# A different order of weight pairs and a different tail in the last chunk of a hybrid encoder block

## The chip, the cores and the metric

The kernel runs as one program on one core of a Trainium2 chip. The metric is the device time of one execution in microseconds (us). Three runs of the kernel before gave 1358.62, 1359.98 and 1359.87 us, with a median of 1359.87 us. One more execution was profiled. Its own time is 1359.19 us, and the trace of it spans 1357.4 us.

## The reference, cut to what matters

The reference is one encoder block on x of 256 tokens by 2048 channels, all in float32. Its last step, the only one that the change touches, is the second half of the feed-forward network, the residual sum and a final RMS norm:

```python
h = _rmsnorm(x, norm_ffn_g[l])
gate, up = jnp.split(jnp.einsum('bsd,df->bsf', h, w_ffn_in[l]), 2, axis=-1)
x = x + jnp.einsum('bsf,fd->bsd', jax.nn.silu(gate) * up, w_ffn_out[l])
...
def _rmsnorm(x, g):
    y = x32 * lax.rsqrt(jnp.mean(x32 * x32, axis=-1, keepdims=True) + EPS)
    return (y * g.astype(F32)).astype(x.dtype)
```

Here w_ffn_out has 5632 rows and 2048 columns. The mean of squares of the final norm goes over the 2048 channels of each token, so no output can be scaled before the last column of its token is summed.

## The kernel before, in words

**Number format.** Every float32 weight is split into two parts: `whi`, a rounded copy made by ScalarE (L68), and `wlo`, the rest, made by VectorE (L69). The activations H were split in the same way earlier. One product is then three matmuls of 128x512 into one PSUM bank: high by high, high by low and low by high (L283 and L284). The middle one needs `wlo`, the other two need only `whi`. The three add into one bank and stand in that order.

**Halves, pairs and lookahead.** Weights come from memory in halves of 128x1024. `Net.take(i)` hands out half i and first has halves up to i + 5 loaded and split (L130 to L133, AHEAD = 3 and two more). SP issues the loads. A load waits until its buffer, used six loads earlier, is free. ScalarE and VectorE split each half in the order in which the halves are taken.

**Two kinds of pairs.** A pair j stands for 2 x 128 rows of the weights. `Quad` (L261) computes two blocks of 512 output columns for both blocks of 128 tokens (tt = 0 and 1). A *plain* pair has two halves and for each of them four products, one into each of the banks N3, P2, E and Q4 (`plain`, L299): 24 matmuls. The banks P2 and N3 hold the two column blocks of tt = 0, Q4 and E those of tt = 1. A *seven* pair uses seven products in place of eight (a scheme after Strassen): 21 matmuls in four quarters (`seven`, L304), of six, six, six and three. For it VectorE also forms sums of weights, L115 ahead of the first quarter, L120 ahead of the second and L124 ahead of the third, besides the four splits L69, the last of them half as wide. Three of the seven products go to the same banks P2, N3 and Q4, and four to banks of their own, P1, Q5, P7 and P6. After the last seven pair, `sums` (L320) and `shared` (L638) work these four banks out on VectorE (L326, L327, L328) and add them to the result `yacc` (L641, twice).

**The last chunk.** The output projection runs in two parts of the rows. The second part has ten pairs and is done for two chunks of 1024 columns, n = 0 and n = 1. The chunk n = 1 is the last work of the kernel on TensorE. Its order of pairs stands in `PLAN_OUT` (L386): 0, 2, 1, 4, 5, 3, 7, 8, 6, 9, of which 2, 4, 5, 7 and 8 are seven pairs. The last two, 6 and 9, are kept out of `Quad.run` (tail = 2) and run by L644 to L647: for tt = 0 all of their products, then for tt = 1. During the first pairs of this chunk VectorE has the end of the chunk n = 0 to do as well: L361, L362, twice L631 and twice L635. The program writes these ahead of the weight splits that the chunk n = 1 asks for itself.

**The tail.** For each tt the two banks are added to `yacc` by VectorE (L650), ScalarE squares and sums each block (L651), VectorE reduces three partial sums, scales them and adds EPS (L558, L559), and `rsqrt_cols` (L211) makes the inverse root by nine small VectorE instructions (L217 to L225, three rounds of two at the end). Then four blocks of 512 columns are scaled, two by VectorE (L658) and two by ScalarE (L661), and SP stores each as it is done (L662).

**What sets the order.** Each engine runs its instructions in a fixed order. A planner sets it ahead of time, on the whole by the order in which the program writes the instructions, with later ones moved ahead where the planner reckons the earlier ones are not ready.

Of the kernel before, what the change touches and what calls it, by code (L numbers as in the profile page):

```python
# [9 lines left out]
F32 = mybir.dt.float32  # L10
# [3 lines left out]
ALU = mybir.AluOpType  # L14
AX = mybir.AxisListType

P = 128
L = 256
D = 2048
# [7 lines left out]
EPS = 1e-6  # L27
# [351 lines left out]
def plan(pairs, seven):  # L379

    return [(j, seven.index(j) if j in seven else None) for j in pairs]
# [1 line left out]

PLAN_IN = plan(range(8), (2, 4, 6))
PLAN_OUT = [[plan(range(12), (2, 4, 6, 7, 9, 10))] * 2,
            [plan(p, (2, 4, 5, 7, 8)) for p in (range(10), (0, 2, 1, 4, 5, 3, 7, 8, 6, 9))]]  # L386
CHUNKS = (6, 5)
RAW_BUFS = 4
HL_BUFS = 4
# [4 lines left out]
def build(nc, tc, a):  # L394
    net = Net(nc, tc, a)
# [37 lines left out]
    with ExitStack() as top:  # L433
# [15 lines left out]
        ss = const.tile([P, 2, 2, 4], F32, name="ss")  # L449
# [63 lines left out]
        for n in range(4):  # L513
# [4 lines left out]
            if n == 0:  # L518
# [3 lines left out]
                fx = sd.enter_context(tc.tile_pool(name="fx", bufs=1))  # L522
# [7 lines left out]
            for tt in range(2):  # L530
                y = yt[:, tt, :]
# [22 lines left out]
        def rms(which, tts, cols):  # L554

            n = len(tts)
            ms = fx.tile([P, n], F32, name="ms", bufs=2)
            nc.vector.tensor_reduce(out=ms, in_=ss[:, which, tts[0]:tts[0] + n, 0:cols], op=ALU.add, axis=AX.X)  # L558
            nc.vector.tensor_scalar(out=ms, in0=ms, scalar1=1.0 / D, scalar2=EPS, op0=ALU.mult, op1=ALU.add)  # L559
            return net.rsqrt_cols(fx, ms, n)  # L560
# [3 lines left out]
        for part in range(2):  # L564
            H = HE = None
            for c in range(CHUNKS[part]):
                q = Quad(net, fx, X2, XE, PLAN_IN, fi_first[c + 6 * part])
                pq, ne = q.parts()
                q.run()
                if c == 0:  # L570
                    if part == 0:
                        inner.close()
                        hpool = sd.enter_context(tc.tile_pool(name="hpool", bufs=1, side="right"))
                        nc.vector.tensor_copy(out=r2, in_=rms(0, (0, 1), 4))
                    H = hpool.tile([P, 24, 512], F32R, name="H")
                    HE = hpool.tile([P, 6, 2, 3, P], F32R, name="HE")
                q.finish(pq, ne)
                for tt in range(2):
                    nc.scalar.activation(out=pq[:, tt, :], in_=pq[:, tt, :], func=AF.Silu, scale=r2[:, tt:tt + 1])
                    nc.vector.scalar_tensor_tensor(out=pq[:, tt, :], in0=ne[:, tt, :], scalar=r2[:, tt:tt + 1],  # L580
                                                   in1=pq[:, tt, :], op0=ALU.mult, op1=ALU.mult)

                def to_h(j, pq=pq, H=H, HE=HE, slots=dict(PLAN_OUT[part][0])):
                    def sink(pt):

                        slot = slots[j]
                        flat = pq[:, j % 2, :].rearrange("p (b t) -> p b t", b=2)
                        nc.scalar.copy(out=flat, in_=pt)
                        hi, lo = H[:, 2 * j:2 * j + 2, 0:L], H[:, 2 * j:2 * j + 2, L:2 * L]
                        nc.scalar.copy(out=hi, in_=flat)  # L590

                        def rest():
                            nc.vector.tensor_tensor(out=lo, in0=flat, in1=hi.bitcast(F32), op=ALU.subtract)
                            if slot is not None:
                                forms(net, fx, flat, HE, slot, H, j)
                        net.later(3 + j % 2, rest)
                    return sink
                net.later(4, lambda pq=pq, c=c, f=to_h: net.turn([[pq[:, tt, L * b:L * (b + 1)] for tt in range(2)] for b in range(2)],
                                                                 [f(2 * c + b) for b in range(2)]))
            for n in range(2):  # L600
                end = part == 1 and n == 1
                q = Quad(net, fx, H, HE, PLAN_OUT[part][n], fo_first[2 * part + n], tail=2 if end else 0)
                if part == 1 and n == 0:

                    x2s.close()
                    gfp = sd.enter_context(tc.tile_pool(name="gfp", bufs=1))
                    yacc = gfp.tile([P, 2, D], F32, name="yacc")
                    gB = gfp.tile([P, D], F32, name="gfB")
                    other = [gfp.tile([P, D], F32, name=f"other{tt}") for tt in range(2)]
                    for tt in range(2):  # L610
                        nc.sync.dma_start(out=yacc[:, tt, :], in_=y_d[tt])
                        nc.sync.dma_start(out=other[tt], in_=p_d[tt])
                    nc.sync.dma_start(out=gB, in_=a["gfin"].partition_broadcast(P))
                    for tt in range(2):
                        net.later(9 + 2 * tt, lambda tt=tt: nc.vector.tensor_tensor(out=yacc[:, tt, :], in0=yacc[:, tt, :],
                                                                                    in1=other[tt], op=ALU.add))
                if not end:
                    pq, ne = q.parts()
                    q.run()
                    q.finish(pq, ne)  # L620
                    if part == 0:
                        def store(n=n, pq=pq, ne=ne):
                            for tt in range(2):
                                for h, t in enumerate((pq, ne)):
                                    c = 1024 * n + 512 * h
                                    nc.sync.dma_start(out=p_d[tt, :, c:c + 512], in_=t[:, tt, :])
                        net.later(2, store)
                    else:
                        for h, t in enumerate((pq, ne)):
                            y = yacc[:, :, 512 * h:512 * (h + 1)]  # L630
                            nc.vector.tensor_tensor(out=y, in0=y, in1=t, op=ALU.add)  # L631
                        for tt in range(2):
                            y = yacc[:, tt, 0:1024]
                            nc.scalar.activation(out=other[tt][:, 0:1024], in_=y, func=AF.Square, accum_out=ss[:, 1, tt, 0:1])
                            nc.vector.tensor_tensor(out=y, in0=y, in1=gB[:, 0:1024], op=ALU.mult)  # L635
                    continue

                def shared(q):  # L638
                    for h, t in enumerate((q.t[:, 1:3, :], q.d)):
                        y = yacc[:, :, 1024 + 512 * h:1536 + 512 * h]  # L640
                        nc.vector.tensor_tensor(out=y, in0=y, in1=t, op=ALU.add)  # L641
                q.run(shared)

                ws = [(net.take(q.first[m] + e), 2 * q.plan[m][0] + e) for m in (-2, -1) for e in range(2)]  # L644
                for tt in range(2):
                    for w, k in ws:
                        q.plain(w, k, (tt,))  # L647
                    for h, name in enumerate((("P2", "N3"), ("Q4", "E"))[tt]):
                        y = yacc[:, tt, 1024 + 512 * h:1536 + 512 * h]
                        nc.vector.tensor_tensor(out=y, in0=q.bank[name], in1=y, op=ALU.add)  # L650
                        nc.scalar.activation(out=other[tt][:, 512 * h:512 * h + 512], in_=y, func=AF.Square,  # L651
                                             accum_out=ss[:, 1, tt, 1 + h:2 + h])

                    r = rms(1, (tt,), 3)
                    for m in (0, 2, 1, 3):
                        y = yacc[:, tt, 512 * m:512 * (m + 1)]
                        if m >= 2:
                            nc.vector.scalar_tensor_tensor(out=y, in0=y, scalar=r[:, 0:1], in1=gB[:, 512 * m:512 * (m + 1)],  # L658
                                                           op0=ALU.mult, op1=ALU.mult)
                        else:  # L660
                            nc.scalar.activation(out=y, in_=y, func=AF.Identity, scale=r[:, 0:1])  # L661
                        nc.sync.dma_start(out=a["out"][tt * P:(tt + 1) * P, 512 * m:512 * (m + 1)], in_=y)  # L662


def phase_a(net, const, ev, psa, ysgu, par, gate_d, sgu_v, tiles, tile_first, sa, left):
# [535 lines left out]
```

## Time and profile before

| | |
|---|---|
| median of three runs | 1359.87 us |
| profiled execution, its own time | 1359.19 us |
| span of its trace | 1357.4 us |
| TensorE (PE) busy | 1340.0 us, 99% |
| weight loads (PEld) busy | 1120.6 us, 83% |
| VectorE (DVE) busy | 1164.2 us, 86% |
| ScalarE (ACT) busy | 796.6 us, 59% |
| chunk n = 1, first and last matmul begin | 1289.95 and 1344.93 us |

All times of the trace count from the start of its span. A row of a timeline gives the begin, the duration, engine, line and operation, output and inputs with their shapes, and how many like instructions in a row were merged into it. An instruction's duration reaches a little past the begin of the next one on its engine, so the pace of a sequence is read from begins.

### The profile page before, as it was taken

The page shows a single profiled execution, that of the slowest core. Times are in us where ns is not written, and L with a number is a line of the kernel's source. Part 1 is how long each engine was busy: PE and PEld are TensorE (multiplying, and loading weights), DVE is VectorE, ACT ScalarE, POOL GpSimd, SP SyncE. Part 2 cuts the span into 40 slices and gives each one's busy share as a digit, 9 for nine tenths or more (in the row PEclk, how much of TensorE's full clock was granted, in tenths as well). Part 3 has the DMA queues.
Part 4 walks back from the last instruction along what each step waited for, and adds up shares of the span by engine and source line. Part 5 has one row for each costly group of instructions (what it writes and reads, how often), then busy time and mean ns, then how long its engine had stood idle before and what let it go on. Part 6 is the DMA issues. An engine that isn't in the chain of part 4 may idle for free.

```text
span 1357.4 us, 17857 instructions
## 1 busy us (share of the span) xinstructions
PE 1340.0 (99%) x6389; PEld 1120.6 (83%) x6389; DVE 1164.2 (86%) x1593; ACT 796.6 (59%) x1034; POOL 0.7 (0%) x6
## 2 busy tenths in 40 slices
PE   9999999999999999999999999999999999999996
PEld 7888888888888888888888888888888888888775
DVE  7887789798889666656898999999999989999998
ACT  7665555455555444455666666666665667665654
POOL 0000000000000000000000000000000000000000
PEclk9999999999999999999999999999999999999998
DMA  8775656556555687676556665666767567558643
GB/s 293 253 241 175 190 179 195 178 170 215 159 179 153 213 342 237 186 233 196 188 188 204 203 209 178 202 201 197 245 209 233 194 192 235 184 186 325 210 165 124
DMA packets 90681, 280.25 MB, mean 206 GB/s; under 512 B 10072, under 2 KB 10976, under 8 KB 89952
## 3 DMA queue, kind: packets, MB, share of 16 engines
q1 hardware_dynamic: 88144, 274.84, 62.7%
q10 hardware_dynamic: 2448, 4.27, 0.8%
q8 instruction: 50, 0.82, 0.2%
q14 instruction: 39, 0.32, 0.1%
HBM read 268.58 MB, written 10.49 MB: 206 GB/s over the span
## 4 chain that ended last, share of the span: by engine, by line
PE 92%; DVE 5%; issue 1%; DMA 1%; ACT 1%; SPq 0%; DVEq 0%; ACTq 0%
PE mm L284 19%; PE mg L284 17%; PE aux L284 10%; PE mm L139 9%; PE mg L173 6%; PE mg L174 6%; PE mg L175 6%; PE mm L141 4%; PE mm L174 2%; PE mm L175 2%; PE mm L173 2%; DVE wlo L69 2%; PE aux L790 2%; PE aux L204 1%; DMA raw<-in_wsv 1%
## 5 line engine op out<-in xcount | busy, mean ns | idle before, releaser
L68 ACT CAST whi<-raw 128x1024 fp32r<-128x1024 f32 (+1 forms) x530 | 523.6, 1002 | 428.1 <-PE mm L284 109.1
L69 DVE TENSOR_TENSOR wlo<-raw,whi 128x1024 fp32r<-128x1024 f32 (+1 forms) x530 | 606.6, 1160 | 152.7 <-ACT whi L68 146.6
L284 PE MATMUL mm<-whi,X 128*128 128x512 f32 x572 | 204.8, 389 | 0.0
L284 PE MATMUL mg<-whi,X 128*128 128x512 f32 x506 | 174.0, 390 | 0.0
L139 PE MATMUL mm<-X,whi 128*128 128x512 f32 x512 | 161.4, 397 | 0.0
L284 PEld LDWEIGHTS mm<-whi,X 128*128 128x128 f32 x572 | 107.4, 188 | 22.3
L141 PEld LDWEIGHTS mm<-X,wlo 128*128 128x128 f32 x512 | 96.3, 188 | 22.4
L284 PEld LDWEIGHTS mg<-whi,X 128*128 128x128 f32 x506 | 95.0, 188 | 20.0 <-DVE yt L532 0.3
L284 PE MATMUL mm<-wlo,X 128*128 128x512 f32 x286 | 111.4, 389 | 0.0
L173 PE MATMUL mg<-whi,X 128*128 128x512 f32 x256 | 101.1, 395 | 0.0
L141 PE MATMUL mm<-X,wlo 128*128 128x256 f32 x512 | 101.0, 278 | 0.0
L174 PE MATMUL mg<-wlo,X 128*128 128x512 f32 x256 | 100.0, 391 | 0.0
L175 PE MATMUL mg<-whi,X 128*128 128x512 f32 x256 | 99.9, 391 | 0.0
L284 PE MATMUL mg<-wlo,X 128*128 128x512 f32 x253 | 98.5, 389 | 0.0
L284 PE MATMUL mm<-whi,H 128*128 128x512 f32 x264 | 95.4, 391 | 0.8 <-ACT whi L68 0.5
L139 PEld LDWEIGHTS mm<-X,whi 128*128 128x128 f32 x512 | 79.1, 189 | 1.0
L68 ACT CAST whi<-racc 128x1024 fp32r<-128x1024 f32 x55 | 58.0, 1054 | 33.1 <-DVE racc L115 16.1
L284 PE MATMUL mg<-whi,H 128*128 128x512 f32 x220 | 76.2, 391 | 0.0
L284 PE MATMUL aux<-whi,XE 128*128 128x512 f32 x198 | 71.7, 389 | 0.0
L115 DVE TENSOR_TENSOR racc<-raw 128x1024 f32<-128x1024 f32 x55 | 67.1, 1220 | 4.1 <-DMA raw<-in_wfi 2.4
L69 DVE TENSOR_TENSOR wlo<-racc,whi 128x1024 fp32r<-128x1024 f32 x55 | 67.2, 1221 | 1.9 <-ACT whi L68 1.6
L284 PEld LDWEIGHTS mm<-wlo,X 128*128 128x128 f32 x286 | 53.7, 188 | 11.1
(286 smaller groups left out, 2285.0 us busy)
## 6 DMA issues: line engine op xcount, KB each, us to landing
raw<-in_wfi SPq DMA_DIRECT2D x143, 512.0 KB, 4.1
raw<-in_wfo SPq DMA_DIRECT2D x66, 512.0 KB, 4.3
raw<-in_wg SPq DMA_DIRECT2D x64, 512.0 KB, 3.6
raw<-in_win SPq DMA_DIRECT2D x64, 512.0 KB, 3.9
raw<-in_wfi SPq DMA_DIRECT2D x66, 256.0 KB, 3.0
raw<-in_wbr SPq DMA_DIRECT2D x32, 512.0 KB, 5.4
raw<-in_wout SPq DMA_DIRECT2D x32, 512.0 KB, 3.8
raw<-in_wfo SPq DMA_DIRECT2D x44, 256.0 KB, 3.3
```

The source lines that it names most:

```text
L68: self.nc.scalar.copy(out=hi, in_=src)
L69: self.nc.vector.tensor_tensor(out=lo, in0=src, in1=hi.bitcast(F32), op=ALU.subtract)
L115: nc.vector.tensor_tensor(out=r[2].rearrange("p (c n) -> p c n", c=2), in0=r[1].rearrange("p (c n) -> p c n", c=2), in1=r[4][:, 512:1024]. ...
L139: nc.tensor.matmul(ps[:, 0:512], lhsT=hi[:, col:col + P], rhs=mov, start=start, stop=False)
L141: nc.tensor.matmul(ps[:, 0:256], lhsT=lo[:, col:col + P], rhs=mov[:, 0:256], start=False, stop=stop)
L173: self.nc.tensor.matmul(ps[tt], lhsT=xh, rhs=wh, start=start, stop=False)
L174: self.nc.tensor.matmul(ps[tt], lhsT=xh, rhs=wl, start=False, stop=False)
L175: self.nc.tensor.matmul(ps[tt], lhsT=xl, rhs=wh, start=False, stop=stop)
L204: self.nc.tensor.transpose(out=pt[:, b, tt * P:(tt + 1) * P], in_=src[tt][:, b * P:(b + 1) * P], identity=self.ident)
L284: self.net.nc.tensor.matmul(ps, lhsT=l, rhs=r, start=(n == 0), stop=(n == self.total[name] - 1))
L790: nc.tensor.matmul(ps[:, ri, :], lhsT=fw[:, m + ri, :], rhs=z, start=(n == 0), stop=(n == 2))
```

## The change

Four edits, all in the chunk n = 1. The order of its pairs becomes 0, 2, 4, 5, 1, 7, 8, 3, 6, 9. In the tail the two banks of a token block are filled one after the other, each by all four halves, and not both by one half after the other. The first two of the three partial sums of squares are reduced, scaled and joined with EPS as soon as the first bank's sum is there, and one instruction adds the third. And of the four output blocks of a token block the two that ScalarE scales are stored from ScalarE's own queue.

```diff
-            [plan(p, (2, 4, 5, 7, 8)) for p in (range(10), (0, 2, 1, 4, 5, 3, 7, 8, 6, 9))]]
+            [plan(p, (2, 4, 5, 7, 8)) for p in (range(10), (0, 2, 4, 5, 1, 7, 8, 3, 6, 9))]]
...
                 for tt in range(2):
-                    for w, k in ws:
-                        q.plain(w, k, (tt,))
                     for h, name in enumerate((("P2", "N3"), ("Q4", "E"))[tt]):
+                        for w, k in ws:
+                            q.mul(name, w, 512 * h, q.at(k, tt))
                         y = yacc[:, tt, 1024 + 512 * h:1536 + 512 * h]
                         nc.vector.tensor_tensor(out=y, in0=q.bank[name], in1=y, op=ALU.add)
                         nc.scalar.activation(out=other[tt][:, 512 * h:512 * h + 512], in_=y, func=AF.Square,
                                              accum_out=ss[:, 1, tt, 1 + h:2 + h])
-
-                    r = rms(1, (tt,), 3)
+                        if h == 0:
+
+                            ms = fx.tile([P, 2], F32, name="ms2", bufs=2)
+                            nc.vector.tensor_reduce(out=ms[:, 0:1], in_=ss[:, 1, tt:tt + 1, 0:2], op=ALU.add, axis=AX.X)
+                            nc.vector.tensor_scalar(out=ms[:, 0:1], in0=ms[:, 0:1], scalar1=1.0 / D, scalar2=EPS,
+                                                    op0=ALU.mult, op1=ALU.add)
+
+                    nc.vector.scalar_tensor_tensor(out=ms[:, 1:2], in0=ss[:, 1, tt, 2:3], scalar=1.0 / D, in1=ms[:, 0:1],
+                                                   op0=ALU.mult, op1=ALU.add)
+                    r = net.rsqrt_cols(fx, ms[:, 1:2], 1)
...
-                        nc.sync.dma_start(out=a["out"][tt * P:(tt + 1) * P, 512 * m:512 * (m + 1)], in_=y)
+                        (nc.sync if m >= 2 else nc.scalar).dma_start(out=a["out"][tt * P:(tt + 1) * P, 512 * m:512 * (m + 1)], in_=y)
```

## Rows read from the trace of the kernel before

**Rows 1.** The page, part 1: busy time, share of the span and instructions of each engine.
```profile
PE 1340.0 (99%) x6389; PEld 1120.6 (83%) x6389; DVE 1164.2 (86%) x1593; ACT 796.6 (59%) x1034; POOL 0.7 (0%) x6
```

**Rows 2.** Windows of the last chunk: stretch and length, busy time of each engine, granted clock, DMA.
```profile
1300.00:1320.00 20.00, 18.33 (x73) 12.68 (x71) 20.00 (x22) 11.24 (x14) 0.00 (x0) 1.00 0.45 150
1320.00:1340.00 20.00, 19.96 (x89) 16.32 (x88) 19.93 (x23) 10.69 (x12) 0.00 (x0) 1.00 0.46 152
```

**Rows 3.** Timeline of DVE over the last chunk: begin, duration, engine, line, operation.
```profile
1289.68 0.69 DVE L326 TENSOR_TENSOR T<-aux,T 128x512 f32<-128x512 f32 x1
1290.28 0.69 DVE L120 TENSOR_TENSOR raw<-racc,raw 128x512 f32<-128x512 f32 x1
...
1300.02 1.83 DVE L69 TENSOR_TENSOR wlo<-raw,whi 128x512 fp32r<-128x512 f32 x2
1301.76 2.36 DVE L635 TENSOR_TENSOR yacc<-yacc,gfB 128x1024 f32<-128x1024 f32 x2
1304.02 1.23 DVE L69 TENSOR_TENSOR wlo<-raw,whi 128x1024 fp32r<-128x1024 f32 x1
...
1311.51 1.23 DVE L115 TENSOR_TENSOR racc<-raw 128x1024 f32<-128x1024 f32 x1
1312.64 1.23 DVE L69 TENSOR_TENSOR wlo<-raw,whi 128x1024 fp32r<-128x1024 f32 x1
1313.78 0.69 DVE L120 TENSOR_TENSOR raw<-racc,raw 128x512 f32<-128x512 f32 x1
...
1316.12 4.10 DVE L69 TENSOR_TENSOR wlo<-raw,whi 128x1024 fp32r<-128x1024 f32 x4
1320.12 1.23 DVE L115 TENSOR_TENSOR racc<-raw 128x1024 f32<-128x1024 f32 x1
...
1331.12 6.37 DVE L69 TENSOR_TENSOR wlo<-raw,whi 128x1024 fp32r<-128x1024 f32 x6
1337.40 0.68 DVE L326 TENSOR_TENSOR T<-aux,T 128x512 f32<-128x512 f32 x1
...
1342.25 1.28 DVE L650 TENSOR_TENSOR yacc<-mm,yacc 128x512 f32<-128x512 f32 x2
```

**Rows 4.** Chain that ended last, the 24 matmuls of tt = 0 in the tail.
```profile
1334.44 5.44 PE mm L284 x24
```

**Rows 5.** Timeline of the tail, all engines, from the last matmul.
```profile
1344.93 0.39 PE L284 MATMUL mg<-whi,H 128*128 128x512 f32 x1
...
1346.61 0.19 ACT L651 ACTIVATION_READ_ACCUMULATOR other<-yacc 128x1 f32 x1
...
1346.96 0.15 DVE L558 TENSOR_REDUCE ms<-ss 128x1 f32<-128x3 f32 x1
...
1348.25 1.41 DVE L658 SCALAR_TENSOR_TENSOR yacc<-yacc,rs_y,gfB 128x512 f32<-128x512 f32 x2
1348.94 4.55 SPq L662 DMA_DIRECT2D out_y<-yacc  x8
...
1350.12 0.21 DVE L225 TENSOR_SCALAR rs_y<-rs_t,rs_y 128x1 f32<-128x1 f32 x1
...
1350.68 0.21 DVE L225 TENSOR_SCALAR rs_y<-rs_t,rs_y 128x1 f32<-128x1 f32 x1
1350.93 1.33 ACT L661 ACTIVATE yacc<-yacc,rs_y 128x512 f32<-128x512 f32 x2 [1.40 <-DVE rs_y L225]
```

**Rows 6.** The stores, line 662: from issue to landing.
```profile
DMA to landing us min/median/max: 2.7/2.7/2.9
```

**Rows 7.** Timeline of ACT in an earlier stage, where ACT stores what it made (L997).
```profile
466.45 0.69 ACT L996 ACTIVATE sq<-mg,rcol 128x512 f32<-128x512 f32 x1 [0.90 <-PE mg L175]
467.17 0.35 ACTq L997 DMA_DIRECT2D gate_d<-sq  x1
467.62 0.69 ACT L996 ACTIVATE sq<-mg,rcol 128x512 f32<-128x512 f32 x1 [0.48 <-ACT sq L996]
```

**Rows 8.** Window after the last matmul, with the granted clock.
```profile
1348.00:1349.00 1.00, 0.00 (x0) 0.00 (x0) 1.00 (x4) 0.81 (x2) 0.00 (x0) 0.53 0.00 0
```

## The prediction

> **What bounds the kernel now.** I read the page first, for the engines' shares. TensorE is busy 99% of the span [rows 1], and read so the order of the weight pairs could not matter. The windows of the last chunk say otherwise. From 1300 to 1320 us VectorE is busy for all of its 20.00 us and TensorE for 18.33 [rows 2], with 73 matmuls against 89 in the next 20 us. There TensorE waits for weights that VectorE splits. The Trainium skill, "Perfetto Trace Analysis", section "Identifying the Most-Contended Engine", calls the busy share of matmuls a poor measure and wants the busy share of weight loads beside it; here that falls from 16.32 to 12.68 us of 20, on the side of the windows. By matmul busy time alone the edit of the order would be worth nothing, which is the second rival below.
>
> The timeline of VectorE shows why. Hardly a pause lies between 1300.02 and 1337.40 us: 20.00 and 19.93 us of the two windows are busy [rows 2, 3]. So the third thing to read is which half of the weights it finishes when, and how much TensorE has to do after that half.
>
> Prices, from begins. A matmul takes 5.44 / 24 = 0.2267 us [rows 4]. On VectorE a full split L69 and a sum L115 take 1.13 each (1312.64 to 1313.78, 1311.51 to 1312.64), L326 takes 0.60 (1289.68 to 1290.28), and L120, of the same length, as much; a half-wide split with a full one takes 1.74 (1300.02 to 1301.76), so 0.60 by itself [rows 3]. A seven pair goes from 1311.51 to the split of pair 3, which is two splits (2.26) before 1320.12, that is to 1317.86: 6.35 us of VectorE [rows 3]. It gives TensorE 21 x 0.2267 = 4.76 us. A plain pair costs VectorE 2.26 and gives TensorE 24 x 0.2267 = 5.44. Seven pairs eat VectorE's lead, plain ones restore it.
>
> The end of TensorE's work is then the largest, over all halves, of (split done) + (matmuls from this half on). Two halves set it. The third quarter of pair 5 is split at 1316.12 + 1.13 = 1317.25 [rows 3]; from it on come 6 + 3 + 24 (pair 3) + 42 (pairs 7, 8) + 48 (pairs 6, 9) = 123 matmuls, 27.9 us: 1345.1. The third quarter of pair 8 is split at 1331.12 + 1.13 = 1332.25 [rows 3]; 9 + 48 = 57 matmuls, 12.9 us: 1345.2. In the trace the last matmul begins at 1344.93 [rows 5] and its 0.23 us end at 1345.16. The rule is met within 0.1 us, from both halves.
>
> **The order of pairs.** In the new order pair 1 stands behind pair 5, and pair 3 behind pair 8. Ahead of the third quarter of pair 5 VectorE has one plain pair less to split: 1317.25 - 2.26 = 1314.99. But behind it TensorE now has 24 matmuls more: 147 x 0.2267 = 33.3, which makes 1348.3. For pair 8: 1332.25 - 2.26 = 1329.99, plus 81 x 0.2267 = 18.36: 1348.35. Both say the same: a plain pair moved behind the binding half comes 2.26 earlier on VectorE and 5.44 later on TensorE, **+3.18 us**. The total of VectorE's work is unchanged, so nothing here is given back. Pair 7's third quarter gives less, (1329.99 - 6.35) + 102 x 0.2267 = 1346.8. The loads move with the pairs: the last half of pair 9 now uses the buffer that pair 8's third quarter leaves at 1330.0, and not one that is free by 1328; it has until about 1339.7, so I price this at nothing. Were the load's cover gone it would be the first rival's case.
>
> `sums` and the L641 adds, 1342.25 - 1337.40 = 4.85 us [rows 3], may begin earlier by the order, but they still stand behind VectorE's splits. Their end is about 1342.2 as before, and as TensorE ends 3.2 us later, they no longer press on tt = 0.
>
> **One bank, then the other.** The number of matmuls is the same. The last bank's add begins 0.4 us after the last matmul in either order, and the other bank's add goes from between two others to 2.72 us earlier (12 matmuls). It gains nothing by itself after the last matmul: before, ScalarE's last read of a sum came at 1346.61 + 0.19 = 1346.80, 1.87 after the last matmul's begin [rows 5], and that is add, square and read of one bank alone. The price of the order is that the first bank needs the last half of pair 9 after 9 matmuls (2.0 us) and not after 18 (4.1 us).
>
> **Mean square made ahead.** Before, from that read (1346.80) to the scaling (1350.93) it took 4.13 us [rows 5]. In this stretch tt = 0's chain lay interleaved with tt = 1's, and its two scalings (from 1348.25, 1.41 us) stood ahead of tt = 1's last rounds. After the change tt = 0's banks are full 5.4 us (24 matmuls) before the end; its chain of some 4 us and its scaling fit beside them. For tt = 1 stay: 0.16 to the first instruction (1346.80 to 1346.96), one instruction where there were two, and `rsqrt_cols` alone. I take 0.25 for each of the three steps to the first round (a step of the rounds is 0.56 / 2 = 0.28, from 1350.12 to 1350.68), 0.22 into the first round, three rounds at 0.56 less the last step's 0.25, and 0.25 to the scaling (1350.68 to 1350.93) [rows 5]. That is 0.16 + 0.50 + 0.22 + 1.42 + 0.25, about 2.55 us: **-1.58 us** against 4.13. Bounds: 0 (tt = 0 lies in the way as before) and -1.9 (only ten small steps at 0.22).
>
> **Half the stores from ScalarE.** Before, SP began its eight stores from 1348.94 and ended issuing at 1353.49, each 0.33 to 0.42; the last begins some 0.4 before that, at 1353.1, and lands 2.7 later at 1355.8 [rows 5, 6]. The scaling of that block had ended at 1350.93 + 1.41 = 1352.34, so SP's queue came 0.76 late. With two queues this wait goes. But a store in ScalarE's queue waits for the scaling ahead of it, and holds the next scaling: in the earlier stage the second of two ACTIVATEs began 467.62 - 466.45 = 1.17 us after the first, and not 0.69 [rows 7]. So ScalarE's second block is ready at 1.17 + 0.69 = 1.86 after the scaling's begin and its store begins at 1.9, against 1353.1 - 1350.93 = 2.17 before: **-0.3 us**. Bounds: -0.76 (both scalings placed first) and +0.5 (ScalarE's stores of tt = 0 also hold the last square of tt = 1, by up to 0.46). The Trainium skill, "DMA: Bandwidth & Descriptors", section "Issuing engines are not separate DMA queues", says that transfers from several engines' queues run on the same 16 DMA engines and that only issue time is saved. It speaks against any gain in the transfers; if two queues did double their rate, the 2.7 us would shrink, and the sum would be up to 1.3 lower. The trace of before has no two queues storing at once.
>
> **Sum.** 1359.19 + 3.18 - 1.58 - 0.3 = **1360.5 us**, against the profiled execution, which lies 0.7 below the median of the runs and inside their spread (1358.62 to 1359.98). That is no change that can be measured: within 0.2% of the median means 1357.15 to 1362.6, about what a measurement of this kernel can tell from no change.
>
> **Rivals.** *The last weights come late (slower).* If the planner puts the last split of pair 9 behind `sums` and L641, because it is written behind them in the new order, VectorE reaches it late: 1329.99 + 0.60 + 5 x 1.13 = 1336.2 for the splits ahead, + 4.85, + 1.13 = 1342.2. TensorE comes to it at 1348.3 - 48 x 0.2267 + 10 x 0.2267 = 1339.7. It waits 2.5 us: 1363.0. It decides as soon as the split ends after 1339.7. For it: the order in which it is written. Against it: at 1290.28 a later-written L120 stands right behind L326 [rows 3], in the gap of a dependent step, and there the split would be ready by 1338.
>
> *The order costs nothing (faster).* If the planner fills TensorE's waits with matmuls of other pairs that need only `whi`, or VectorE's stream closes up, only the tail counts: 1359.19 - 1.9 = 1357.3, with the larger bounds of the tail 1356.5. For it: TensorE's 99%. Against it: the rule above meets the end of before twice within 0.1 us, with whatever filling the planner did there.
>
> *The clock falls.* Behind pair 2 TensorE now meets a seven pair. Pair 2's last split ends at 1300.62, and pair 4's first must wait for L115 (1.13) and both L635 (to 1304.02): it ends at 1305.15 [rows 3]. So TensorE has nearly nothing from 1301.1 to 1305.2, about 4 us. The granted clock was 0.53 in 1348 to 1349 [rows 8], some 3 us after the last matmul, so it can fall to 1.2 GHz here. A seven pair then takes 9.5 us, 3.2 beyond VectorE's 6.35; pair 4's third quarter is not binding by 1.6 ((1314.99 - 6.35) + 168 x 0.2267 = 1346.7), so one seven pair at that clock costs 1.6: 1362.1, and two 1365. Against it: the fill-in matmuls of pair 4 that need only `whi` break the gap.
>
> *The mean square isn't ahead.* If the planner again lays tt = 0's chain or its scalings beside tt = 1's, the 1.58 is lost: 1362.1. Its first sum needs L641, done by 1342.2, and its second bank fills at 1342.9, so there are 5.4 us for it; against.
>
> **How the numbers follow.** Forecast 50% (1359.2 to 1362.0), order free 22%, weights late 10%, clock 10%, mean square not ahead 8%. Half of the second case lies below 1357.15, and little of the first: faster 0.14. Weights late, half of the clock's case and a part of the forecast's upper edge lie above 1362.6: slower 0.22. Within 0.2%: 0.64. The range for 8 in 10 goes from 1356.8, in the second case, to 1363.4, past the first rival.
>
> **What would show it.** Right: TensorE's last matmul begins near 1348.1; between 1301 and 1318 it is idle some 3 us more; the split of pair 8's third quarter ends near 1330.0, and 81 matmuls follow without a gap; tt = 1's scaling begins 4.4 after the last matmul's begin and not 6.0; the span ends 10.6 after it and not 12.5. Wrong: a last matmul at 1345 or earlier (the rule of halves fails), or at 1350 and later with a wait for `wlo` of pair 9, or a granted clock under 1 near 1305.

## The result, and the profile after

The kernel after takes **1374.24 us** (median of 4 runs, 1373.55 to 1375.32) against 1359.59 us for the kernel before, run beside it on the same chip (4 runs, 1358.62 to 1359.98). The ratio is 1.0109, with a 95% interval of 1.0097 to 1.0122: slower by 14.7 us. The forecast was 1360.5, within 1356.8 to 1363.4. The profiled execution of after took 1374.32 us, its span is 1372.5.

Part 1 of the page of after shows no reason, only a longer span:

```profile
PE 1353.4 (99%) x6389; PEld 1121.0 (82%) x6389; DVE 1167.5 (85%) x1595; ACT 795.9 (58%) x1034; POOL 0.7 (0%) x6
```

TensorE executes the same 6389 matmuls in 13.4 us more of busy time [rows 1], at the same share of 99%. VectorE's timeline of after says when the time was lost (begin, duration, engine, line, operation):

```profile
1303.45 0.68 DVE L326 TENSOR_TENSOR T<-aux,T 128x512 f32<-128x512 f32 x1
...
1317.80 1.21 DVE L69 TENSOR_TENSOR wlo<-raw,whi 128x1024 fp32r<-128x1024 f32 x1
...
1340.86 1.21 DVE L69 TENSOR_TENSOR wlo<-racc,whi 128x1024 fp32r<-128x1024 f32 x1
1342.00 0.67 DVE L124 TENSOR_TENSOR raw<-raw 128x512 f32<-128x512 f32 x1
1342.60 7.49 DVE L69 TENSOR_TENSOR wlo<-raw,whi 128x1024 fp32r<-128x1024 f32 x7
1350.01 0.67 DVE L326 TENSOR_TENSOR T<-aux,T 128x512 f32<-128x512 f32 x1
1350.61 1.21 DVE L69 TENSOR_TENSOR wlo<-raw,whi 128x1024 fp32r<-128x1024 f32 x1
```

The first L326 of this stretch began at 1289.68 before [rows 3] and begins at 1303.45 now, **13.77 us later, before any matmul of the chunk n = 1 that the change touches**. The first matmul of the chunk is as late, 1303.71 against 1289.95. Up to there the instructions stand in the same order on every engine. I then took the begins of the same instructions in both traces, pair by pair. The difference is 0.58 us up to 647 us on before's time (0.54 of it there by 57 us), grows to 7.70 by 902, stands still until 1025, and grows to 13.73 by 1236. The two stretches in which it grows are the input projections of the feed-forward network, whose matmuls read the tile X2. In the stretch where it stands still they read H.

The windows of the matmul line L284 show it in one view. Columns: stretch and length, busy time of matmuls and of weight loads, with counts, granted clock, DMA share, GB/s. Before:

```profile
665.00:900.00 235.00, 231.85 (x1019) 190.60 (x1018) 1.00 0.63 202
925.00:1030.00 105.00, 105.00 (x465) 86.99 (x464) 1.00 0.69 224
1045.00:1230.00 185.00, 182.48 (x802) 150.03 (x801) 1.00 0.63 202
```

After:

```profile
665.00:900.00 235.00, 231.85 (x990) 185.10 (x989) 1.00 0.62 196
925.00:1030.00 105.00, 105.00 (x465) 86.94 (x464) 1.00 0.69 220
1045.00:1230.00 185.00, 182.48 (x779) 145.76 (x778) 1.00 0.60 194
```

The busy time is the same to 0.01 us and the clock is the full one, but where X2 is read fewer matmuls fit: 990 for 1019, 779 for 802. On H both have 465. From begin to begin a matmul on X2 takes 233.3 ns after and 226.7 before. Eleven chunks of 183 matmuls are 2013 matmuls, and 2013 x 6.6 ns = 13.3 us. With the 0.5 us of the kernel's start that is the 13.77. (The start isn't the change's: e1 and e8 below, with the same instructions up to the last chunk, differ by 0.6 us at 648 us.)

What can the change do to X2? It defines a new small tile, `ms2`, of two floats with two buffers, which take 32 bytes of a partition each, 64 in all. Its pool stands ahead of X2's in memory, so everything behind it moved: X2 from byte 94464 of the partition (a multiple of 256) to 94528, XE with it, and VectorE's tile racc. H, HE and the weight buffers stayed.

**The last chunk by itself**, with 13.77 taken off, is another story. TensorE's begins of after, where the prediction saw a gap:

```profile
1314.87 0.39 PE L284 MATMUL mg<-whi,H 128*128 128x512 f32 x1
1317.08 0.73 PE L284 MATMUL aux<-whi,HE 128*128 128x512 f32 x2 [1.82 <-ACT whi L68]
1319.07 0.50 PE L284 MATMUL aux<-wlo,H 128*128 128x512 f32 x1 [1.26 <-DVE wlo L69]
...
1321.90 0.63 PE L284 MATMUL aux<-whi,HE 128*128 128x512 f32 x1
1322.33 0.63 PE L284 MATMUL aux<-wlo,HE 128*128 128x512 f32 x1
```

The two waits are the gap (1301.3 to 1305.3 on before's time), and after it the step is 0.43 us: the granted clock has fallen. The windows of after (columns of [rows 2]) put numbers to it; the third and fourth answer to the two of [rows 2], 14 us later:

```profile
1318.00:1322.00 4.00, 2.57 (x7) 1.60 (x8) 4.00 (x5) 1.58 (x3) 0.00 (x0) 0.73 0.24 73
1321.00:1323.40 2.40, 2.40 (x6) 1.92 (x7) 2.40 (x4) 1.56 (x2) 0.00 (x0) 0.53 0.56 207
1314.00:1334.00 20.00, 16.11 (x61) 11.78 (x61) 20.00 (x22) 12.15 (x16) 0.00 (x0) 0.91 0.49 167
1334.00:1354.00 20.00, 19.95 (x88) 16.18 (x88) 19.96 (x22) 11.55 (x14) 0.00 (x0) 1.00 0.49 162
```

In the stretch with the gap TensorE is busy for 16.11 us where it was 18.33, 2.2 us less (some 3 were predicted), and in the next one for 19.95.

And the tail of after, all engines, from the last matmul, to be held against [rows 5]:

```profile
1361.37 1.42 DVE L666 SCALAR_TENSOR_TENSOR yacc<-yacc,rs_y,gfB 128x512 f32<-128x512 f32 x2
1361.38 0.39 PE L284 MATMUL mg<-whi,H 128*128 128x512 f32 x1
...
1362.70 0.68 DVE L650 TENSOR_TENSOR yacc<-mg,yacc 128x512 f32<-128x512 f32 x1
...
1363.95 0.19 ACT L651 ACTIVATION_READ_ACCUMULATOR other<-yacc 128x1 f32 x1
1364.17 0.16 DVE L660 SCALAR_TENSOR_TENSOR ms<-ss,ms 128x1 f32<-128x1 f32 x1 [0.79 <-ACT other L651]
...
1366.42 1.33 ACT L669 ACTIVATE yacc<-yacc,rs_y 128x512 f32<-128x512 f32 x2 [2.28 <-DVE rs_y L225]
1366.42 1.42 DVE L666 SCALAR_TENSOR_TENSOR yacc<-yacc,rs_y,gfB 128x512 f32<-128x512 f32 x2
1367.17 0.97 ACTq L670 DMA_DIRECT2D out_y<-yacc  x2
1367.20 1.00 SPq L670 DMA_DIRECT2D out_y<-yacc  x2
```

The last add L650 waits behind the two scalings L666 of tt = 0. VectorE is one after the other at 1362.70, with no idle time between, and the last matmul began 1.32 us before, where 0.4 would do. So the last matmul is at 1347.61 on before's time (1348.1 predicted), the scaling of tt = 1 comes 5.04 us after it (4.4 predicted) and the span ends 11.1 us after it (10.6 predicted).

### The profile page after: what moved, and what is told of

The parts are those of the page before. It is cut to its first block, busy times and chain, and to the rows that moved or that the text cites. A ratio compares the mean times of both kernels' runs of the same rounds, so it can differ in the third digit from the quotient of the medians.

```text
span 1372.5 us, 17859 instructions
## 1 busy us (share of the span) xinstructions
PE 1353.4 (99%) x6389; PEld 1121.0 (82%) x6389; DVE 1167.5 (85%) x1595; ACT 795.9 (58%) x1034; POOL 0.7 (0%) x6
## 4 chain that ended last, share of the span: by engine, by line
PE 94%; DVE 3%; ACT 1%; DMA 1%; issue 0%; SPq 0%; DVEq 0%; ACTq 0%
PE mm L284 20%; PE mg L284 18%; PE aux L284 10%; PE mm L139 9%; PE mg L173 6%; PE mg L174 6%; PE mg L175 6%; PE mm L141 4%; PE mm L174 2%; PE mm L175 2%; PE mm L173 2%; PE aux L798 2%; PE aux L204 1%; DVE wlo L69 1%; ACT whi L68 1%; DMA raw<-in_wsv 1%
## 5 line engine op out<-in xcount | busy, mean ns | idle before, releaser
L284 PE MATMUL mm<-whi,X 128*128 128x512 f32 x572 | 208.2, 395 | 0.0
L284 PE MATMUL mg<-whi,X 128*128 128x512 f32 x506 | 177.0, 395 | 0.0
L284 PEld LDWEIGHTS mm<-whi,X 128*128 128x128 f32 x572 | 107.4, 188 | 26.1
L284 PEld LDWEIGHTS mg<-whi,X 128*128 128x128 f32 x506 | 95.0, 188 | 23.3 <-DVE yt L532 0.3
L284 PE MATMUL mm<-wlo,X 128*128 128x512 f32 x286 | 113.0, 395 | 0.0
L284 PE MATMUL mg<-wlo,X 128*128 128x512 f32 x253 | 100.0, 395 | 0.0
L284 PE MATMUL mm<-whi,H 128*128 128x512 f32 x264 | 96.0, 393 | 0.9 <-ACT whi L68 0.9
L284 PE MATMUL mg<-whi,H 128*128 128x512 f32 x220 | 76.3, 390 | 0.0
L284 PE MATMUL aux<-whi,XE 128*128 128x512 f32 x198 | 72.9, 395 | 0.0
L284 PEld LDWEIGHTS mm<-wlo,X 128*128 128x128 f32 x286 | 53.7, 188 | 13.0
```

What stands on the lines that cost most here:

```text
L284: self.net.nc.tensor.matmul(ps, lhsT=l, rhs=r, start=(n == 0), stop=(n == self.total[name] - 1))
```

## The experiments

Two theories stood after the comparison. **Place:** the new tile moves X2, and a matmul whose operands start at other offsets takes longer. **Work:** something that the new order or the new tail does costs the time in some way that the comparison hides. Medians follow with the range and the number of runs, ratios with their 95% interval.

**e1, the change with the old addresses.** The new tile takes the name and so the room of one that is there already.

```diff
-                            ms = fx.tile([P, 2], F32, name="ms2", bufs=2)
+                            ms = fx.tile([P, 2], F32, name="ms", bufs=2)
```

> The changed kernel, with its new small tile ms2 given the name of an old one (ms), so that it takes that one's place: all instructions and their order stay, and X2, XE and racc lie where they lay before the change. Theory A (place): the 64 bytes of ms2 moved the 32 KB tile X2, which TensorE loads as stationary operand in the feed-forward input stage, from 94464 to 94528, and there each matmul got 6.6 ns slower. Then the pitch in that stage is 226.7 ns again, and the time is 1374.2 - 13.2 = 1361.0 us, or less if the first 0.5 us of the lag is chance. Theory B (the instructions): something in the new tail or order costs it; then it stays at 1374.

1360.64 us (1360.27 to 1361.66, n = 11), ratio 1.0010 (1.0001 to 1.0019). The matmuls on X2 are back at 226.7 ns, as its windows show:

```profile
665.00:900.00 235.00, 231.85 (x1019) 190.53 (x1018) 1.00 0.63 202
...
1045.00:1230.00 185.00, 182.48 (x802) 149.93 (x801) 1.00 0.63 202
```

So 13.6 us of the loss are the place, and the rest of the change costs 1.2 us against the runs of before beside it (0.1 to 2.6 by the interval).

**e2, the place without the change.** The kernel before, with 64 unused bytes ahead of X2.

```diff
                 fx = sd.enter_context(tc.tile_pool(name="fx", bufs=1))
+                fx.tile([P, 16], F32, name="shift")
```

> The kernel before, with one unused tile of 64 bytes ahead of X2, XE and racc, and nothing else. Theory A: pitch 233.3 ns in the feed-forward input stage, +13.2 us: 1372.8 us. Theory B: no change, 1359.6 us.

1372.93 us (1372.39 to 1373.04, n = 4), ratio 1.0099 (1.0085 to 1.0113), with 233.3 ns on X2 and as few matmuls in the first window as after has:

```profile
665.00:900.00 235.00, 231.86 (x990) 185.31 (x989) 1.00 0.62 196
```

The place alone costs 13.5 us: as the cause of the large loss "work" is out. The matmuls on H stay at 226.7 ns although racc has moved in this stage too, so racc isn't the cause.

**e3 and e4, 128 bytes.** The kernel after with 64 bytes more ahead of X2, in pool fx (e3: racc at 128 as well) or only in X2's own pool (e4: racc stays at 64).

```diff
+                fx.tile([P, 16], F32, name="shift")        # e3, behind the pool fx
+                x2pool.tile([P, 16], F32, name="shift")    # e4, behind the pool x2pool
```

> The changed kernel with ms2 and one more unused tile of 64 bytes, so that X2, XE and racc lie 128 bytes behind their old place. Theory A in the form that a start at a multiple of 128 bytes is what counts: 226.7 ns, 1361 us. Theory A in the form that 256 counts, or theory B: 1374 us.

> The changed kernel with 64 unused bytes more between racc and X2: racc stays 64 bytes off, X2 and XE are 128 bytes off. If X2 and XE (what TensorE loads) are what counts: 226.7 ns, 1361 us. If racc (what VectorE and ScalarE read) counts: 233.3 ns, 1374 us.

e3: 1372.79 us (1372.32 to 1373.23, n = 4), ratio 1.0099 (1.0085 to 1.0112). e4: 1372.84 us (1372.12 to 1373.24, n = 4), the same ratio and interval. The step is 232.7 and 232.4 ns. A multiple of 128 doesn't bring the speed back, and where racc lies makes no difference.

**e5, 256 bytes.** The line of e2 with `[P, 64]`.

> The kernel before, with an unused tile of 256 bytes ahead of X2, XE and racc (and of pq and ne). If a start of the stationary operand at a multiple of 256 bytes is what counts: pitch 226.7 ns in the feed-forward input stage, 1359.5 us. If the old place itself counts (or the distance to the weights' buffers): slower than 226.7 ns, about 1372.

1359.57 us (1359.04 to 1360.17, n = 8), ratio 1.0001 (0.9991 to 1.0011). The windows have 1019, 465 and 802 matmuls again, at 226.7 ns. X2 has moved, by a whole 256 bytes, and it costs nothing.

**e10, 32 bytes.** The line of e2 with `[P, 8]`.

> The kernel before, with an unused tile of 32 bytes ahead of X2, XE and racc. If any start off a multiple of 256 bytes costs the same: about 233 ns on X2, 1372.5 us. If the cost grows or falls with the offset: another pitch between 227 and 240 ns.

One run: 1372.39 us, 233.3 ns, 780 matmuls in the third window. Half of the offset costs as much as the whole.

**e6, the other operand.** 64 bytes ahead of the weight buffers, which moves four of the six by 64 (the other two lie on the other side of the memory), and 192 more ahead of X2, which so moves by 256.

```diff
+        net.ws.tile([P, 16], F32, name="shift0")
...
+                fx.tile([P, 48], F32, name="shift")
```

> The kernel before, with 64 unused bytes ahead of the weights' buffers (two of three whi, wlo and raw then start 64 bytes off a multiple of 256) and 192 more behind them, so that X2 lies at +256. In lines 173 to 175 and 284 the weights are the moving operand, in lines 139 and 141 the stationary one. If only the stationary operand's start counts: lines 173 and 284 keep 226.7 ns, lines 139 and 141 get slower for two thirds of the halves. If the moving operand's start counts: line 284 gets slower on H and X2 alike, by about two thirds of 6.6 ns. If neither: no change.

One run: 1372.84 us. I had expected this only in part: the matmuls on H are slow on average as well now, and so are those whose weights lie in the two buffers that didn't move.

**e9, both.** The first line of e6 alone: four weight buffers, X2, XE and racc at 64; two weight buffers and H at 0.

> The kernel before, with 64 unused bytes ahead of the weights' buffers and nothing behind them: two of three weight buffers, X2, XE and racc all start 64 bytes off a multiple of 256; H, HE and M stay. If only the distance between the two operands counts, line 284 on X2 is as fast as before (226.7 ns) for two of three halves. If each operand's own start counts, it is slower than 226.7 ns throughout, 231 or more, and about 1372 to 1385 us.

One run: 1371.3 us. From the begins of the matmuls, sorted by where their operands lie in the program that is built (X2 and H with their sums XE and HE, steps without a pause up to 1262 us); the last column counts from the last change of the starts, since matmuls on moved and on unmoved weight buffers alternate:

```
start modulo 256: weights / X2 or H     ns from begin to begin: all     from the 11th on
e9   64 / 64  on X2                     228.0  (1333 steps)             226.8  (526)
e9    0 / 64  on X2                     233.3  (660)                    233.2  (68)
e9   64 /  0  on H                      230.9  (417)                    230.9  (151)
e9    0 /  0  on H                      231.2  (179)                    226.6  (14)
e6   64 /  0  on X2                     230.5  (1333)                   230.1  (526)
e6    0 /  0  on X2                     231.1  (660)                    226.7  (68)
```

The first two rows say that it is the starts of the two operands against each other. The rows with 0 / 0 seem to speak against that, but their last column doesn't: a stretch on unmoved buffers is at most twelve matmuls long here, its second to fourth step take some 232.5 ns on average, and from the 11th on the step is 226.7 again. So what is slow there is an after-effect of the change from one pair of starts to another, not the pair 0 / 0.

**e12, everything by 64.** The kernel before with its two filler tiles changed, so that all weight buffers, X2, XE, H and HE start 64 bytes later, and none against another.

```diff
-        const.tile([P, 40], F32, name="const_pad")
+        const.tile([P, 56], F32, name="const_pad")
...
-        edge.tile([P, 56], F32, name="edge_pad")
+        edge.tile([P, 40], F32, name="edge_pad")
```

> The kernel before with the two filler tiles of its edges changed by 64 bytes per partition (const_pad 40 to 56 floats on the left side, edge_pad 56 to 40 on the right), so that every operand of every matmul, weights and stationary operands alike, starts 64 bytes later and none against another. If only the starts of the two operands against each other count, a step stays near 226.7 to 227.7 ns (the latter is what the pairs with both operands 64 bytes on showed in the run before) and the time between 1359.5 and 1365. If each operand's own start counts, the steps go to 233 ns in all stages, X2 and H alike, and the time to 1373 or far above (6000 matmuls at 6.6 ns are 40 us, so up to 1400). Windows of L284 on X2 and on H: x1019, x465, x802 for the one, x990, x451, x780 for the other.

1359.43 us (1359.08 to 1359.92, n = 8), ratio 0.9999 (0.9988 to 1.0011). No operand starts at a multiple of 256 any more, and the windows are those of before:

```profile
665.00:900.00 235.00, 231.85 (x1018) 190.61 (x1018) 1.00 0.63 202
925.00:1030.00 105.00, 105.00 (x465) 87.01 (x464) 1.00 0.68 223
1045.00:1230.00 185.00, 182.49 (x803) 149.98 (x802) 1.00 0.63 203
```

So it is the starts against each other that count, and no multiple of anything by itself.

**e7, the new order alone.** The kernel before with the one line of `PLAN_OUT`.

```diff
-            [... (range(10), (0, 2, 1, 4, 5, 3, 7, 8, 6, 9))]]
+            [... (range(10), (0, 2, 4, 5, 1, 7, 8, 3, 6, 9))]]
```

> The kernel before with the new order of pairs alone; all tiles lie where they lay. By the rule of halves: last matmul 3.2 us later, 1359.5 + 3.2 = 1362.7 us; up to 1.3 less if the later end alone already lets the mean square of tt = 0 finish ahead (its first adds no longer press on tt = 1), 1361.4. If the order costs nothing: 1359.5.

1361.32 us (1360.62 to 1361.82, n = 11), ratio 1.0012 (1.0003 to 1.0021): +1.8 us.

**e8, the new tail alone.** e1 with the old order.

> The changed kernel with the old order of pairs, and ms2 in the place of the old ms, so that all tiles lie where they lay: one bank after the other, mean square ahead and stores from two queues alone. By the sum of the tail: 1359.5 - 1.9 = 1357.6 us. If sums and L641 on VectorE, which in the old order end only 2.9 us before the last matmul does, keep the mean square of tt = 0 from being ahead: some 1358.5 to 1359.2.

1358.55 us (1358.16 to 1359.36, n = 11), ratio 0.9994 (0.9986 to 1.0003): -0.9 us, with an interval that touches no change. VectorE's timeline shows what holds the gain down:

```profile
1347.32 0.14 DVE L217 TENSOR_SCALAR rs_t<-ms 128x1 int32<-128x1 int32 x1
...
1347.69 1.42 DVE L666 SCALAR_TENSOR_TENSOR yacc<-yacc,rs_y,gfB 128x512 f32<-128x512 f32 x2
...
1349.32 0.21 DVE L225 TENSOR_SCALAR rs_y<-rs_t,rs_y 128x1 f32<-128x1 f32 x1
```

The chain of tt = 1 has begun (L217), then come the two scalings of tt = 0, and only then its first round ends: 2.00 us from L217, where the same steps in e1 take 0.69, so 1.3 lost.

**e11, plain pairs early.** By the rule of halves the opposite order should help: the pairs in their natural order, with pair 1 ahead of 2, 3 ahead of 4 and 6 ahead of 7, and only pair 9 for the tail; the new tail, the old addresses.

```diff
-            [... (range(10), (0, 2, 4, 5, 1, 7, 8, 3, 6, 9))]]
+            [... (range(10), range(10))]]
...
-                q = Quad(..., tail=2 if end else 0)
+                q = Quad(..., tail=1 if end else 0)
...
-                ws = [... for m in (-2, -1) for e in range(2)]
+                ws = [... for m in (-1,) for e in range(2)]
```

> The changed kernel with ms2 in the old ms's place, and the order of pairs turned the other way: 0 to 9 in their natural order, so that the plain pairs 3 and 6 stand ahead of the binding seven pairs and only pair 9 in the tail. By the rule of halves a plain pair moved ahead of the binding half makes the end 3.2 us earlier: pair 8's third quarter split at 1332.25 + 2.26 = 1334.5, and 33 matmuls (7.5) behind it: last matmul ends at 1342.0 and not 1345.2. The sums and L641 on VectorE still end at 1342.2, so the four adds of the tail follow them to 1344.7, and the scaling of tt = 1 begins at 1348.1 to 1349.3, where in the run of the tail alone it began at 1350.69: 1358.55 - 2.6 to - 1.4 = 1356.0 to 1357.2 us. If the order of pairs doesn't matter once VectorE is the bound: 1358.5.

1358.30 us (1357.37 to 1358.62, n = 11), ratio 0.9991 (0.9982 to 1.0000). It has the lowest median of all that ran, 1.2 us below before at an interval that ends at no change, and is a good 1 us short of what was expected. TensorE did its part: in 1300 to 1320 it is busy for 19.95 us with 87 matmuls, where [rows 2] had 18.33 and 73, and the last matmul begins at 1342.14, the end 1342.0 of the rule within 0.4. What is late next is VectorE:

```profile
1340.10 2.35 DVE L641 TENSOR_TENSOR yacc<-yacc,T 128x1024 f32<-128x1024 f32 x2
1342.37 1.28 DVE L650 TENSOR_TENSOR yacc<-mm,yacc 128x512 f32<-128x512 f32 x2
...
1347.07 0.33 DVE L225 TENSOR_SCALAR rs_y<-rs_t,rs_y 128x1 f32<-128x1 f32 x2
...
1347.50 1.40 DVE L666 SCALAR_TENSOR_TENSOR yacc<-yacc,rs_y,gfB 128x512 f32<-128x512 f32 x2
1348.82 0.21 DVE L225 TENSOR_SCALAR rs_y<-rs_t,rs_y 128x1 f32<-128x1 f32 x1
```

All four adds L650 stand behind L641, which ends when TensorE does. The chains of both tt then run side by side, and the scalings of tt = 0 hold a round of tt = 1 again, for 1348.82 - 1347.07 - 0.56 = 1.2 us.

## Why the prediction was wrong

**The step that failed.** The prediction took the change for one of the last chunk and counted nothing outside it ("four edits", each with its price there). It named the mean square's new instructions and gave the new tile `ms2` that they write no price at all. That tile's place cost 13.2 us by the begins (13.77 - 0.58), in two stages that the change doesn't touch. No rival held it, so the range didn't either. e1 (tile without the place: the time is back) and e2 (place without the change: the time is lost) show it from both sides. The trace of before could have warned of the place only indirectly. The kernel's own filler tiles, `const_pad` and `edge_pad`, could have warned directly: nobody pads a constant pool by 160 bytes for nothing.

**The terms of the last chunk.** Their sum was +1.3 us; e1 measured +1.2. That was luck: the terms erred in both directions, as begins in the traces show (times in us, the end of a span known to 0.1; before's own are in [rows 5] and in the table of the profile):

| kernel | first matmul of the chunk | to the last one | from there to the scaling of tt = 1 | from there to the end of the span |
|---|---|---|---|---|
| before | 1289.95 | 54.98 | 6.00 | 6.47 |
| after | 1303.71 | 57.67 | 5.04 | 6.08 |
| e1, old addresses | 1290.53 | 58.14 | 5.04 | 5.99 |
| e7, order alone | 1290.42 | 57.65 | 5.35 | 6.28 |
| e8, tail alone | 1289.96 | 55.03 | 5.70 | 6.01 |
| e11, plain early | 1290.08 | 52.06 | 7.48 | 6.68 |

*Order, +3.18 predicted:* +2.69 in after, +2.67 in e7. The split of pair 8's third quarter ended at 1342.60 + 1.13 - 13.77 = 1329.96, where 1329.99 was predicted. But the rule of halves named the wrong wait. It counts every matmul from this half on, and the first ones need only `whi`: two of them, at 1342.20 and 1343.47, run ahead of the end of that split, so 79 and not 81 stand behind it. With them 1329.96 + 79 x 0.2267 = 1347.87; measured 1361.38 + 0.23 - 13.77 = 1347.84. Yet the first matmul that reads this split begins at 1344.38, 0.65 us after its end, so TensorE doesn't wait for it. Its last wait, with 84 matmuls and no pause behind it from 1342.54 on, is for the rounded copy `whi` of the same quarter, which ScalarE ends at 1342.15. In before the last wait is at 1320.27, with 109 matmuls left, for the split that ends the four of [rows 3] from 1316.12: one of pair 3, a plain pair. Neither half that the prediction named was the last to hold TensorE there, and that the rule met the end from both within 0.1 us was luck. The weight loads that waited, before and after:

```profile
1320.27 0.19 PEld L284 LDWEIGHTS mg<-wlo,H 128*128 128x128 f32 x1 [0.47 <-DVE wlo L69]
...
1342.20 0.19 PEld L284 LDWEIGHTS mm<-whi,H 128*128 128x128 f32 x1 [0.48 <-ACT whi L68]
```

*Clock:* what the rival described happened. The gap came where it was said, and the clock fell to near 1.2 GHz behind it: 0.53 in a window of after, above. It cost after nothing that set the end, since there was a pause later, the one that ends at 1342.54. In the profiled execution of e1 it lasted longer:

```profile
1306.00:1312.00 6.00, 6.00 (x14) 4.48 (x15) 6.00 (x7) 3.47 (x4) 0.00 (x0) 0.50 0.56 164
```

There 162 matmuls follow from 1312.11 without a pause, so the low clock set the end, 0.47 us later than in after. The rival priced one seven pair at 1.6. Whether this explains the spread of e1's runs (1360.27 to 1361.66) wasn't traced.

*Mean square ahead, -1.58 predicted:* -0.96. The new chain is as short as was worked out: L660 to the scaling takes 1366.42 - 1364.17 = 2.25, for which the steps gave 2.39. What failed is "its scaling fit beside them". tt = 0's two scalings begin at 1361.37, in the same 0.01 us as the last matmul, and hold the last add for 1362.70 - 1361.38 - 0.42 = 0.90 us (in before the last add began 0.42 after the last matmul). With them out of the way the gain would have been 1.86, near the bound of the prediction. In e8 and e11 the same scalings fall into tt = 1's rounds and cost 1.3 and 1.2. It's this one piece of 1.4 us, whose place nothing in the change sets, that ate into the gain in after, e1, e8 and e11.

*Order alone, better than its matmuls:* e7 ends +1.83 and not +2.67, since a later end of TensorE lets tt = 0's chain finish ahead of it: 5.35 for 6.00, with the old tail. So part of the mean square's gain belongs to the order, and the new tail on the new order brings 1361.32 - 1360.64 = 0.7 by the medians, which their intervals don't tell from nothing.

*Stores, -0.3 predicted:* -0.4 in after (6.08 for 6.47), -0.5 in e1. ScalarE's queue took both stores behind both scalings (1367.17, above), the better of the bounds for this. The last issue ends 1367.20 + 1.00 - 1366.42 = 1.78 us after the scaling's begin, where it was 1353.49 - 1350.93 = 2.56, so 0.8 us of issue time were saved, and about half of it went back behind the issue. Some stores took longer to land with two queues, in the row of L670 that answers to [rows 6] (the trace has the landing of only three of the eight stores, before and after):

```profile
DMA to landing us min/median/max: 2.7/3.0/3.6
```

The Trainium skill, "DMA: Bandwidth & Descriptors", section "Issuing engines are not separate DMA queues", says that DMAs of several engines run on the same 16 DMA engines and that only issue time is saved. This row agrees.

*Weights late, order free:* neither. The last split of pair 9 stands at 1350.61, right behind the first L326 and ahead of the rest of `sums`, in the gap of a dependent step, which is the reason that the prediction gave against the first. The second is excluded by the +2.67 of e7.

## What to carry to other kernels

Read every new tile in a diff as a move of all tiles allocated behind it, however small it is, and ask which of them are operands of the matmuls that fill the kernel; take the room of a tile that is there, or pad so that the starts of weights and stationary operands stay a multiple of 256 bytes apart, as in e5 and e12. When a kernel is slower, first align the begins of the same instructions in both traces: it shows in which stage the time went, while the engine's busy share stays at 99% and hides it. A long instruction without a set place, such as a scaling that is off the path, falls into the path as soon as the path gets shorter; give it its place as part of the change.

## What the runs showed of the hardware that I had not expected

A 128x512 matmul on fp32r operands, back to back at a granted clock of 1.00, took 226.7 ns where both operands start at multiples of 256 bytes or both 64 bytes beyond one (before, e5, e12). It took 233.3 ns with the stationary operand 32 or 64 bytes further on than the moving one (e10, e2, after) and 232.4 to 232.7 with 128 (e3, e4). With the moving operand, the weights, 64 bytes further on it took 230.1 to 230.9 (e6, e9). 233.3 is 2.9% more per matmul, and 1% of this kernel. The Trainium skill, "SBUF — State Buffer", section "Operand start alignment", says that an operand may start at any multiple of its element size, and that this is about legality and not speed. The kernels with starts 32, 64 and 128 bytes off did run, and their times add the speed.

Where the starts changed against each other every few matmuls (e6, e9), the steps on operands that agree were slow too, 231.1 to 231.5 ns on average with both at 0, and back at 226.7 only from the 11th after the change. Open stays why the after-effect lasts that long, and why it matters which of the two operands is further on. VectorE's and ScalarE's work on a tile 64 bytes off isn't enough to slow a matmul: in e2 racc was moved, and the matmuls on H beside it took 226.8.
